# Linear attention on one core: 4 KB runs for K and V as for Q, a second matmul over 128 rows, and output one group behind

## The chip, the cores and the metric

The kernel runs on one core of one Trainium2 chip. The metric is the device time of one execution in microseconds (us), and a kernel's time is the median of several executions. The profile is one execution; its span, from the first to the last instruction, is about 1.8 us shorter than the time of the same execution. A ratio "to before" is the mean time of one kernel's runs over the mean of the other's runs of the same rounds, so it is not quite the ratio of the medians quoted beside it.

Engines: PE multiplies matrices (PEld loads its weights), DVE and ACT do elementwise work, POOL here mostly issues transfers, SP issues a few. HBM is the memory that holds the inputs and the output, SBUF the one that loads fill and stores empty, PSUM the one that PE writes its results to. A "run" of 4 KB is a contiguous stretch in HBM.

## The reference, cut to what matters

```python
# Q, K, V: 8 x 12 x 512 x 64, float32 (96 heads of 512 rows)
Q_feat = np.maximum(0, Q) + 1
K_feat = np.maximum(0, K) + 1
KV = np.einsum('bhkd,bhkv->bhdv', K_feat, V)            # first matmul
K_sum = np.sum(K_feat, axis=2)
numerator = np.einsum('bhqd,bhdv->bhqv', Q_feat, KV)    # second matmul
denominator = np.einsum('bhqd,bhd->bhq', Q_feat, K_sum)
out = numerator / (denominator[:, :, :, None] + 1e-10)
```

## The kernel before

Eight heads form a group, and there are twelve groups. Loads cast float32 to bf16 on the way. V gets a column of ones, so that the first matmul also gives the sum of K's features. Q's features are transposed on PE, and ACT copies the transposes from PSUM to SBUF (`qt`). After the second matmul DVE takes a reciprocal of the denominators and multiplies: one "pair" per PSUM tile, four pairs a group. What the argument touches (cut):

```python
def features(g):                      # DVE: K, then Q; ACT: V
    for h in range(2):
        feature(kf[:, h]..., k_raw[:, h:NP:2])
        nc.scalar.copy(out=va[:, h]..., in_=v_raw[:, h:NP:2])
    feature(qf..., q_raw)
def kv_and_transpose(g):
    # 32 matmuls over 64 rows -> kva_ps; two ACT casts to kva
    for half in range(2):
        qt_ps = psum_qt.tile([P, C, P], BF16, name="qt_ps")   # a tile for each half
        for c in range(C):
            nc.tensor.transpose(qt_ps[:, c, :], qf[:, half * C + c, :, :], identity)
        nc.scalar.copy(out=qt[:, :, :, half], in_=qt_ps)
def output(g):
    # 64 matmuls, 64 rows, 65 moving columns; four pairs of reciprocal and multiply on DVE
    ...
for it in range(NG + 2):
    if it < NG:           features(it)
    if 1 <= it < NG + 1:  kv_and_transpose(it - 1)
    if it >= 2:           output(it - 2)
    if it + IN_BUFS < NG: load(it + IN_BUFS)
    if it - LAG >= 0:     store(it - LAG)        # LAG = 3
```

Of the kernel before, what the change touches and what calls it, by code (L numbers as in the profile page):

```python
# [8 lines left out]
FP32 = mybir.dt.float32  # L9
BF16 = mybir.dt.bfloat16  # L10
ALU = mybir.AluOpType

BANK = 512
VP = 130
IN_BUFS = 4
OUT_BUFS = 6
LAG = 3


@with_exitstack  # L20
def kernel(
    ctx: ExitStack,
    tc: tile.TileContext,
    Q: bass.AP,
    K: bass.AP,
    V: bass.AP,
    out: bass.AP,
):






    nc = tc.nc

    B, H, S, D = Q.shape
    P = 128
    C = 8
    C2 = 2 * C  # L40
    NPAIR = B * H * S // (P * C)
    NP = 4
    NG = NPAIR // NP
    D1 = D + 1
    W = 2 * D + 1

    def view(t, c):
        return t.flatten_outer_dims().rearrange("(n p c) d -> p n c d", p=P, c=c)

    q_dram = view(Q, C2)  # L50
    k_dram = view(K, C)
    v_dram = view(V, C)
    o_dram = view(out, C)

    const = ctx.enter_context(tc.tile_pool(name="const", bufs=1))
    head_pool = ctx.enter_context(tc.tile_pool(name="head_pool", bufs=1))
    in_pool = ctx.enter_context(tc.tile_pool(name="in_pool", bufs=IN_BUFS))
    feat_pool = ctx.enter_context(tc.tile_pool(name="feat", bufs=2))
    mid_pool = ctx.enter_context(tc.tile_pool(name="mid", bufs=3))
    out_pool = ctx.enter_context(tc.tile_pool(name="out_pool", bufs=OUT_BUFS))  # L60
    recip_pool = ctx.enter_context(tc.tile_pool(name="recip", bufs=4))
    psum_qt = ctx.enter_context(tc.tile_pool(name="psum_qt", bufs=2, space=bass.MemoryType.PSUM))
    psum_kva = ctx.enter_context(tc.tile_pool(name="psum_kva", bufs=1, space=bass.MemoryType.PSUM))
    psum_out = ctx.enter_context(tc.tile_pool(name="psum_out", bufs=2, space=bass.MemoryType.PSUM))

    identity = const.tile([P, P], BF16, name="identity")
    NV = 2
    v_aug = [const.tile([P, 2, C, VP], BF16, name=f"v_aug{i}") for i in range(NV)]

    raw = {}  # L70
    feat = {}
    mid = {}
    outs = {}

    def load(g):
        first = g == 0
        k_raw = (head_pool if first else in_pool).tile(
            [P, NP, C, D], FP32 if first else BF16, name="k_raw"
        )
        v_raw = in_pool.tile([P, NP, C, D], BF16, name="v_raw")  # L80
        q_raw = in_pool.tile([P, 2, C2, D], BF16, name="q_raw")
        (nc.sync if first else nc.gpsimd).dma_start(  # L82
            out=k_raw, in_=k_dram[:, g * NP : g * NP + NP]
        )
        nc.gpsimd.dma_start(out=v_raw, in_=v_dram[:, g * NP : g * NP + NP])  # L85
        nc.gpsimd.dma_start(out=q_raw, in_=q_dram[:, g * 2 : g * 2 + 2])  # L86
        raw[g] = (k_raw, v_raw, q_raw)

    def store(g):
        nc.gpsimd.dma_start(out=o_dram[:, g * NP : g * NP + NP], in_=outs.pop(g))  # L90

    def feature(dst, src):
        nc.vector.tensor_scalar(  # L93
            out=dst, in0=src, scalar1=1.0, scalar2=1.0, op0=ALU.add, op1=ALU.max
        )

    def features(g):
        k_raw, v_raw, q_raw = raw.pop(g)
        kf = feat_pool.tile([P, 2, C, 2, D], BF16, name="kf")
        qf = feat_pool.tile([P, C2, 2, D], BF16, name="qf")  # L100
        va = v_aug[g % NV]
        for h in range(2):
            feature(kf[:, h].rearrange("p c n d -> p n c d"), k_raw[:, h:NP:2])
            nc.scalar.copy(  # L104
                out=va[:, h].rearrange("p c (n x) -> p n c x", n=2)[:, :, :, 0:D],
                in_=v_raw[:, h:NP:2],
            )
        feature(qf.rearrange("p c n d -> p n c d"), q_raw)
        feat[g] = (kf, qf)

    def kv_and_transpose(g):
        kf, qf = feat.pop(g)
        va = v_aug[g % NV]
        kva_ps = psum_kva.tile([P, 2, BANK], FP32, name="kva_ps")
        for h in range(2):
            for c in range(C):
                for j in range(2):
                    nc.tensor.matmul(  # L118
                        kva_ps[:, j, h * W : h * W + W],
                        lhsT=kf[64 * j : 64 * j + 64, h, c, :, :],  # L120
                        rhs=va[64 * j : 64 * j + 64, h, c, 0:W],
                        start=(c == 0),
                        stop=(c == C - 1),
                    )
        kva = mid_pool.tile([P, 2, 2, D1 + 1], BF16, name="kva")
        for n in range(2):
            nc.scalar.copy(  # L127
                out=kva[64 * n : 64 * n + 64, :, :, 0:D1],
                in_=kva_ps[64 * n : 64 * n + 64, :, 0 : 2 * W].rearrange(
                    "p j (h x) -> p j h x", h=2  # L130
                )[:, :, :, D * n : D * n + D1],
            )

        qt = mid_pool.tile([P, C, P, 2], BF16, name="qt")
        for half in range(2):
            qt_ps = psum_qt.tile([P, C, P], BF16, name="qt_ps")
            for c in range(C):
                nc.tensor.transpose(qt_ps[:, c, :], qf[:, half * C + c, :, :], identity)  # L138
            nc.scalar.copy(out=qt[:, :, :, half], in_=qt_ps)  # L139
        mid[g] = (kva, qt)  # L140

    def output(g):
        kva, qt = mid.pop(g)
        o_sb = out_pool.tile([P, NP, C, D], FP32, name="o_sb")
        for h in range(2):
            ops = [psum_out.tile([P, 2, BANK], FP32, tag="o_ps", name="o_ps") for _ in range(2)]
            for c in range(C):
                off = (c % 4) * D1
                for n in range(2):
                    for j in range(2):  # L150
                        b = 2 * h + j
                        nc.tensor.matmul(  # L152
                            ops[n][64 * j : 64 * j + 64, c // 4, off : off + D1],
                            lhsT=qt[64 * n : 64 * n + 64, c, 32 * b : 32 * b + 32, :],
                            rhs=kva[64 * n : 64 * n + 64, j, h, 0:D1],
                            start=True,
                            stop=True,
                        )
            for n in range(2):
                cells = ops[n][:, :, 0 : 4 * D1].rearrange("p b (r x) -> p b r x", x=D1)  # L160
                den = cells[:, :, :, 0:1] if n else cells[:, :, :, D:D1]
                num = cells[:, :, :, 1:D1] if n else cells[:, :, :, 0:D]
                recip = recip_pool.tile([P, 2, 4, 1], FP32, name="recip")
                nc.vector.reciprocal(out=recip, in_=den)  # L164
                nc.vector.tensor_tensor(  # L165
                    out=o_sb[:, 2 * n + h].rearrange("p (b r) d -> p b r d", b=2),
                    in0=num,
                    in1=recip.to_broadcast([P, 2, 4, D]),
                    op=ALU.mult,
                )  # L170
        outs[g] = o_sb

    with tc.manual_schedule():
        for g in range(IN_BUFS):
            load(g)
            if g == 0:
                make_identity(nc, identity)
                for t in v_aug:
                    nc.gpsimd.memset(t[:, :, :, D : D + 1], 1.0)  # L179
        for it in range(NG + 2):  # L180
            if it < NG:
                features(it)
            if 1 <= it < NG + 1:
                kv_and_transpose(it - 1)
            if it >= 2:
                output(it - 2)
            if it + IN_BUFS < NG:
                load(it + IN_BUFS)
            s = it - LAG
            if s >= 0:  # L190
                store(s)
        for s in range(NG + 2 - LAG, NG):
            store(s)


# [28 lines left out]
```

## Time and profile before

| | before |
|---|---|
| time, median of 4 | 132.04 us (130.11 to 132.31) |
| span of the profile | 129.8 us |
| busy: PE, DVE, ACT | 59.0, 57.7, 62.6 us |
| mean granted PE clock | 0.686 |

The prediction below shows the main lines. In the page's table of costliest groups the columns are line, engine, operation, output from input, count, then busy us and mean ns of one, then the idle time before them and what ended it.

```profile
L104 ACT COPY v_aug<-v_raw 128x1024 bf16<-128x1024 bf16 x24 | 24.1, 1056 | 48.6 <-DMA v_raw<-in_V_dram 48.6
...
L139 ACT COPY qt<-qt_ps 128x1024 bf16<-128x1024 bf16 x24 | 29.5, 1298 | 0.4
```

ACT stands idle 48.6 us in front of its V copies, and what ends that idle time is V's load: the engines wait for data. In front of the qt copies ACT is idle only 0.4 us in the whole kernel. The transposes that they read are nearly always there already.

### The profile page before, as it was taken

How to read it: one execution, taken by the hardware profiler on the slowest of the kernel's cores; microseconds unless marked ns; L12 is line 12 of the kernel's file. 1: busy time of each engine (PE TensorE's matmuls, PEld its weight loads, DVE VectorE, ACT ScalarE, POOL GpSimd, SP SyncE). 2: the span in 40 equal slices, each digit the busy share in tenths (PEclk: the TensorE clock that was granted, in tenths of full speed). 3: DMA queues.
4: the chain of work that ended last, by engine and by line, in shares of the span. 5: the costliest groups of instructions: out<-in, count | busy, mean ns of one | idle time of the engine just before them, and what ended most of it. 6: DMA issues, size and time to landing. Idle time of an engine off the chain costs nothing.

```text
span 129.8 us, 3048 instructions
## 1 busy us (share of the span) xinstructions
PE 59.0 (46%) x1344; PEld 50.5 (39%) x1344; DVE 57.7 (44%) x132; ACT 62.6 (48%) x73; POOL 36.1 (28%) x55
## 2 busy tenths in 40 slices
PE   0008309208758292864939119409606802933200
PEld 0007209107647191753828009308505701922100
DVE  0222212057374775727577077066227407567700
ACT  3023086590966939296690590391095096270000
POOL 6972224222332242224224222422231200202020
PEclk9999965555686959555595865875785685595555
DMA  2999999999999999999999999999999999999853
GB/s 93 321 204 195 210 194 204 210 206 211 205 209 208 209 207 206 210 207 207 277 302 207 253 331 205 231 350 191 218 347 223 212 357 418 420 417 360 341 218 121
DMA packets 19213, 32.17 MB, mean 248 GB/s; under 512 B 768, under 2 KB 12544, under 8 KB 19200
## 3 DMA queue, kind: packets, MB, share of 16 engines
q0 software_dynamic: 18672, 30.94, 106.3%
q1 hardware_dynamic: 528, 1.05, 2.1%
q8 instruction: 10, 0.16, 0.5%
q14 instruction: 3, 0.02, 0.0%
HBM read 37.75 MB, written 12.58 MB: 388 GB/s over the span
## 4 chain that ended last, share of the span: by engine, by line
DMA 72%; issue 19%; POOL 4%; POOLq 1%
DMA out_dram<-o_sb 31%; DMA k_raw<-in_K_dram 16%; DMA q_raw<-in_Q_dram 15%; DMA v_raw<-in_V_dram 9%; POOL out_dram L90 2%; POOLq L219 1%; POOL q_raw L86 1%; POOL k_raw L82 0%; POOL v_raw L85 0%; POOL identity masks.py:199 0%; POOL identity masks.py:197 0%; POOL v_aug L179 0%; POOLq L90 0%; POOLq L86 0%; POOLq L208 0%
## 5 line engine op out<-in xcount | busy, mean ns | idle before, releaser
L104 ACT COPY v_aug<-v_raw 128x1024 bf16<-128x1024 bf16 x24 | 24.1, 1056 | 48.6 <-DMA v_raw<-in_V_dram 48.6
L152 PE MATMUL o_ps<-kva,qt 64*64 64x65 bf16 x768 | 17.3, 229 | 46.9 <-DVE o_sb L165 45.8
L165 DVE TENSOR_TENSOR o_sb<-o_ps,recip 128x512 f32<-128x512 f32 x48 | 33.2, 691 | 1.6
L152 PEld LDWEIGHTS <-qt 64*64 64x64 bf16 x768 | 12.7, 137 | 52.0 <-DVE o_sb L165 48.9
L139 ACT COPY qt<-qt_ps 128x1024 bf16<-128x1024 bf16 x24 | 29.5, 1298 | 0.4
L118 PE MATMUL kva_ps<-v_aug,kf 64*128 64x129 bf16 x384 | 22.3, 302 | 15.4 <-ACT v_aug L104 10.1
L93 DVE TENSOR_SCALAR qf<-q_raw 128x2048 bf16<-128x2048 bf16 x12 | 8.3, 694 | 42.2 <-DMA q_raw<-in_Q_dram 42.2
L118 PEld LDWEIGHTS <-kf 64*128 64x128 bf16 x384 | 19.1, 137 | 16.2 <-issue 15.6
L138 PE MATMUL qt_ps<-identity,qf 128*128 128x128 bf16 x192 | 21.7, 303 | 0.1
L90 POOL DMA_DIRECT2D out_dram<-o_sb x12 | 9.3, 774 | 38.2 <-DVE o_sb L165 19.6
L138 PEld LDWEIGHTS <-qf 128*128 128x128 bf16 x192 | 18.8, 142 | 2.6 <-issue 2.2
L93 DVE TENSOR_SCALAR kf<-k_raw 128x1024 bf16<-128x1024 bf16 (+1 forms) x24 | 9.8, 450 | 11.2 <-DMA k_raw<-in_K_dram 11.1
L164 DVE RECIPROCAL recip<-o_ps 128x8 f32<-128x8 f32 x48 | 9.6, 201 | 10.5 <-PE o_ps L152 10.5
L85 POOL DMA_DIRECT2D v_raw<-in_V_dram x12 | 9.1, 759 | 17.0 <-ACT kva L127 5.4
L82 POOL DMA_DIRECT2D k_raw<-in_K_dram x11 | 8.6, 786 | 16.7 <-DVE kf L93 6.6
L86 POOL DMA_DIRECT2D q_raw<-in_Q_dram x12 | 8.4, 702 | 15.9 <-DMA k_raw<-in_K_dram 9.0
L127 ACT CAST kva<-kva_ps 64x260 bf16<-64x260 f32 x24 | 8.8, 367 | 3.5 <-PE kva_ps L118 3.4
L104 ACT ACT_TABLE_LOAD x1 | 1.3, 1283 | 0.7 <-PEq L208 0.7
masks.py:199 POOL TENSOR_SCALAR_AFFINE_SELECT identity<-identity 128x128 bf16<-128x128 bf16 x1 | 0.3, 287 | 0.1
masks.py:197 POOL MEMSET identity<- 128x128 bf16 x1 | 0.2, 244 | 0.0
L179 POOL MEMSET v_aug<- 128x16 bf16 x2 | 0.2, 175 | 0.0
L208 POOL MEMSET const-float32-0.0<- 128x1 f32 x1 | 0.1, 99 | 0.2 <-issue 0.2
(3 smaller groups left out, 0.3 us busy)
## 6 DMA issues: line engine op xcount, KB each, us to landing
out_dram<-o_sb POOLq DMA_DIRECT2D x12, 1024.0 KB, 20.0
v_raw<-in_V_dram POOLq DMA_DIRECT2D x12, 512.0 KB, 19.7
q_raw<-in_Q_dram POOLq DMA_DIRECT2D x12, 512.0 KB, 19.8
k_raw<-in_K_dram POOLq DMA_DIRECT2D x11, 512.0 KB, 19.7
k_raw<-in_K_dram SPq DMA_DIRECT2D x1, 1024.0 KB, 5.0
```

The source lines that it names most:

```text
L85: nc.gpsimd.dma_start(out=v_raw, in_=v_dram[:, g * NP : g * NP + NP])
L86: nc.gpsimd.dma_start(out=q_raw, in_=q_dram[:, g * 2 : g * 2 + 2])
L90: nc.gpsimd.dma_start(out=o_dram[:, g * NP : g * NP + NP], in_=outs.pop(g))
L93: nc.vector.tensor_scalar(out=dst, in0=src, scalar1=1.0, scalar2=1.0, op0=ALU.add, op1=ALU.max)
L104: nc.scalar.copy(out=va[:, h].rearrange("p c (n x) -> p n c x", n=2)[:, :, :, 0:D], in_=v_raw[:, h:NP:2],)
L118: nc.tensor.matmul(kva_ps[:, j, h * W : h * W + W], lhsT=kf[64 * j : 64 * j + 64, h, c, :, :], rhs=va[64 * j : 64 * j + 64, h, c, 0:W], st ...
L127: nc.scalar.copy(out=kva[64 * n : 64 * n + 64, :, :, 0:D1], in_=kva_ps[64 * n : 64 * n + 64, :, 0 : 2 * W].rearrange("p j (h x) -> p j h x ...
L138: nc.tensor.transpose(qt_ps[:, c, :], qf[:, half * C + c, :, :], identity)
L139: nc.scalar.copy(out=qt[:, :, :, half], in_=qt_ps)
L152: nc.tensor.matmul(ops[n][64 * j : 64 * j + 64, c // 4, off : off + D1], lhsT=qt[64 * n : 64 * n + 64, c, 32 * b : 32 * b + 32, :], rhs=kv ...
L164: nc.vector.reciprocal(out=recip, in_=den)
L165: nc.vector.tensor_tensor(out=o_sb[:, 2 * n + h].rearrange("p (b r) d -> p b r d", b=2), in0=num, in1=recip.to_broadcast([P, 2, 4, D]), op ...
```

## The change

Its intent: longer contiguous runs for the loads of K and V (4 KB as for Q), a second matmul that uses all 128 rows by placing two heads' weights on a block diagonal, and a shorter end, by making output one group behind instead of two and stores two behind instead of three. The core of the diff (cut and condensed; memsets and some shapes left out):

```diff
-IN_BUFS = 4
+IN_BUFS = 5
+AHEAD = 4
-LAG = 3
+LAG = 2
-    k_dram = view(K, C)
-    v_dram = view(V, C)
+    k_dram = view(K, C2)
+    v_dram = view(V, C2)
-    psum_qt, psum_kva, psum_out (2, 1 and 2 buffers)
+    psum = ctx.enter_context(tc.tile_pool(name="psum", bufs=4, space=bass.MemoryType.PSUM))
+    def keys_values(g):
+        # K features and V copies by halves, 64 matmuls over 32 rows, four casts to kva_diag
+    def queries(g):
+        qt_ps = psum.tile([P, 2, C, P], BF16, tag="ps", name="qt_ps")    # one tile for both halves
+        for half in range(2):
+            feature(qf[:, cs]..., q_raw[:, :, cs])
+            for c in range(C):
+                nc.tensor.transpose(qt_ps[:, half, c, :], qf[:, half * C + c, :, :], identity)
+            nc.scalar.copy(out=qt[:, :, :, half], in_=qt_ps[:, half])
     def output(g):
-        # lhsT=qt[64 * n : 64 * n + 64, c, ...], rhs=kva[64 * n : 64 * n + 64, j, h, 0:D1]
+        # lhsT=qt[:, c, ...], rhs=kva[:, b]  (128 rows, 130 columns, zeros off the diagonal)
-            features(it); kv_and_transpose(it - 1); output(it - 2); load(it + IN_BUFS); store(it - LAG)
+            load(g + AHEAD); store(g - LAG); keys_values(g); output(g - 1); queries(g)
```

More of the change, by code (lines that the diff above doesn't have):

```diff
@@ L13 @@
 BANK = 512
-VP = 130
-IN_BUFS = 4
+IN_BUFS = 5
 OUT_BUFS = 6
-LAG = 3
+AHEAD = 4
+LAG = 2
 @with_exitstack
@@ L44 @@
     D1 = D + 1
-    W = 2 * D + 1
+    W = 2 * D1
     def view(t, c):
@@ L61 @@
     recip_pool = ctx.enter_context(tc.tile_pool(name="recip", bufs=4))
-    psum_qt = ctx.enter_context(tc.tile_pool(name="psum_qt", bufs=2, space=bass.MemoryType.PSUM))
-    psum_kva = ctx.enter_context(tc.tile_pool(name="psum_kva", bufs=1, space=bass.MemoryType.PSUM))
-    psum_out = ctx.enter_context(tc.tile_pool(name="psum_out", bufs=2, space=bass.MemoryType.PSUM))
+    psum = ctx.enter_context(tc.tile_pool(name="psum", bufs=4, space=bass.MemoryType.PSUM))
     identity = const.tile([P, P], BF16, name="identity")
     NV = 2
-    v_aug = [const.tile([P, 2, C, VP], BF16, name=f"v_aug{i}") for i in range(NV)]
+    v_aug = [const.tile([P, C2, W], BF16, name=f"v_aug{i}") for i in range(NV)]
+    kva_diag = [const.tile([P, 4, 2, D1], BF16, name=f"kva_diag{i}") for i in range(NV)]
     raw = {}
-    feat = {}
-    mid = {}
+    qts = {}
     outs = {}
@@ L77, in load @@
         k_raw = (head_pool if first else in_pool).tile(
-            [P, NP, C, D], FP32 if first else BF16, name="k_raw"
+            [P, 2, C2, D], FP32 if first else BF16, name="k_raw"
         )
-        v_raw = in_pool.tile([P, NP, C, D], BF16, name="v_raw")
+        v_raw = in_pool.tile([P, 2, C2, D], BF16, name="v_raw")
         q_raw = in_pool.tile([P, 2, C2, D], BF16, name="q_raw")
         (nc.sync if first else nc.gpsimd).dma_start(
-            out=k_raw, in_=k_dram[:, g * NP : g * NP + NP]
+            out=k_raw, in_=k_dram[:, g * 2 : g * 2 + 2]
         )
-        nc.gpsimd.dma_start(out=v_raw, in_=v_dram[:, g * NP : g * NP + NP])
+        nc.gpsimd.dma_start(out=v_raw, in_=v_dram[:, g * 2 : g * 2 + 2])
         nc.gpsimd.dma_start(out=q_raw, in_=q_dram[:, g * 2 : g * 2 + 2])
@@ L89, in store @@
     def store(g):
-        nc.gpsimd.dma_start(out=o_dram[:, g * NP : g * NP + NP], in_=outs.pop(g))
+        o_sb = outs.pop(g)
+        o_to = o_dram[:, g * NP : g * NP + NP]
+        if g < NG - 1:
+            nc.gpsimd.dma_start(out=o_to, in_=o_sb)
+            return
+        for h in range(2):
+            nc.sync.dma_start(out=o_to[:, h:NP:2], in_=o_sb[:, h:NP:2])
     def feature(dst, src):
@@ L95, in feature @@
         )
-    def features(g):
-        k_raw, v_raw, q_raw = raw.pop(g)
-        kf = feat_pool.tile([P, 2, C, 2, D], BF16, name="kf")
-        qf = feat_pool.tile([P, C2, 2, D], BF16, name="qf")
-        va = v_aug[g % NV]
-        for h in range(2):
-            feature(kf[:, h].rearrange("p c n d -> p n c d"), k_raw[:, h:NP:2])
-            nc.scalar.copy(
-                out=va[:, h].rearrange("p c (n x) -> p n c x", n=2)[:, :, :, 0:D],
-                in_=v_raw[:, h:NP:2],
-            )
-        feature(qf.rearrange("p c n d -> p n c d"), q_raw)
-        feat[g] = (kf, qf)
@@ L111, in kv_and_transpose @@
-    def kv_and_transpose(g):
-        kf, qf = feat.pop(g)
-        va = v_aug[g % NV]
-        kva_ps = psum_kva.tile([P, 2, BANK], FP32, name="kva_ps")
-        for h in range(2):
+    def keys_values(g):
+        k_raw, v_raw, _ = raw[g]
+        kf = feat_pool.tile([P, C2, 2, D], BF16, name="kf")
+        va = v_aug[g % NV]
+        kva_ps = [psum.tile([P, 2, BANK], FP32, tag="ps", name="kva_ps") for _ in range(2)]
+        for half in range(2):
+            cs = slice(half * C, half * C + C)
+            feature(kf[:, cs].rearrange("p c n d -> p n c d"), k_raw[:, :, cs])
+            nc.scalar.copy(
+                out=va[:, cs].rearrange("p c (n x) -> p n c x", n=2)[:, :, :, 0:D],
+                in_=v_raw[:, :, cs],
+            )
+            for c in range(half * C, half * C + C):
+                for b in range(4):
+                    ps = slice(32 * b, 32 * b + 32)
+                    nc.tensor.matmul(
+                        kva_ps[b // 2][:, b % 2, 0:W],
+                        lhsT=kf[ps, c, :, :],
+                        rhs=va[ps, c, :],
+                        start=(c == 0),
+                        stop=(c == C2 - 1),
+                    )
+        kva = kva_diag[g % NV]
+        for n in range(2):
+            ps = slice(64 * n, 64 * n + 64)
+            for h in range(2):
+                nc.scalar.copy(
+                    out=kva[ps, 2 * h : 2 * h + 2, n, :],
+                    in_=kva_ps[h][ps, :, D1 * n : D1 * n + D1],
+                )
@@ new lines, in queries @@
+    def queries(g):
+        _, _, q_raw = raw.pop(g)
+        qf = feat_pool.tile([P, C2, 2, D], BF16, name="qf")
+        qt = mid_pool.tile([P, C, P, 2], BF16, name="qt")
+        qt_ps = psum.tile([P, 2, C, P], BF16, tag="ps", name="qt_ps")
+        for half in range(2):
+            cs = slice(half * C, half * C + C)
+            feature(qf[:, cs].rearrange("p c n d -> p n c d"), q_raw[:, :, cs])
+            for c in range(C):
+                nc.tensor.transpose(qt_ps[:, half, c, :], qf[:, half * C + c, :, :], identity)
+            nc.scalar.copy(out=qt[:, :, :, half], in_=qt_ps[:, half])
+        qts[g] = qt
@@ L116, in kv_and_transpose, with output @@
+    def output(g):
+        kva = kva_diag[g % NV]
+        qt = qts.pop(g)
+        o_sb = out_pool.tile([P, NP, C, D], FP32, name="o_sb")
+        for h in range(2):
+            ops = [psum.tile([P, 2, BANK], FP32, tag="ps", name="o_ps") for _ in range(2)]
             for c in range(C):
                 for j in range(2):
+                    b = 2 * h + j
                     nc.tensor.matmul(
-                        kva_ps[:, j, h * W : h * W + W],
-                        lhsT=kf[64 * j : 64 * j + 64, h, c, :, :],
@@ L121, in kv_and_transpose @@
-                        rhs=va[64 * j : 64 * j + 64, h, c, 0:W],
-                        start=(c == 0),
-                        stop=(c == C - 1),
-                    )
-        kva = mid_pool.tile([P, 2, 2, D1 + 1], BF16, name="kva")
-        for n in range(2):
-            nc.scalar.copy(
-                out=kva[64 * n : 64 * n + 64, :, :, 0:D1],
-                in_=kva_ps[64 * n : 64 * n + 64, :, 0 : 2 * W].rearrange(
-                    "p j (h x) -> p j h x", h=2
-                )[:, :, :, D * n : D * n + D1],
-            )
@@ L134, in kv_and_transpose @@
-        qt = mid_pool.tile([P, C, P, 2], BF16, name="qt")
-        for half in range(2):
-            qt_ps = psum_qt.tile([P, C, P], BF16, name="qt_ps")
-            for c in range(C):
-                nc.tensor.transpose(qt_ps[:, c, :], qf[:, half * C + c, :, :], identity)
-            nc.scalar.copy(out=qt[:, :, :, half], in_=qt_ps)
-        mid[g] = (kva, qt)
-    def output(g):
-        kva, qt = mid.pop(g)
-        o_sb = out_pool.tile([P, NP, C, D], FP32, name="o_sb")
-        for h in range(2):
-            ops = [psum_out.tile([P, 2, BANK], FP32, tag="o_ps", name="o_ps") for _ in range(2)]
-            for c in range(C):
-                off = (c % 4) * D1
-                for n in range(2):
-                    for j in range(2):
-                        b = 2 * h + j
-                        nc.tensor.matmul(
-                            ops[n][64 * j : 64 * j + 64, c // 4, off : off + D1],
-                            lhsT=qt[64 * n : 64 * n + 64, c, 32 * b : 32 * b + 32, :],
-                            rhs=kva[64 * n : 64 * n + 64, j, h, 0:D1],
-                            start=True,
-                            stop=True,
-                        )
-            for n in range(2):
-                cells = ops[n][:, :, 0 : 4 * D1].rearrange("p b (r x) -> p b r x", x=D1)
-                den = cells[:, :, :, 0:1] if n else cells[:, :, :, D:D1]
-                num = cells[:, :, :, 1:D1] if n else cells[:, :, :, 0:D]
-                recip = recip_pool.tile([P, 2, 4, 1], FP32, name="recip")
-                nc.vector.reciprocal(out=recip, in_=den)
-                nc.vector.tensor_tensor(
-                    out=o_sb[:, 2 * n + h].rearrange("p (b r) d -> p b r d", b=2),
-                    in0=num,
-                    in1=recip.to_broadcast([P, 2, 4, D]),
@@ new lines, in output @@
+                        ops[c // 4][64 * j : 64 * j + 64, c // 2 % 2, (c % 2) * W : (c % 2) * W + W],
+                        lhsT=qt[:, c, 32 * b : 32 * b + 32, :],
+                        rhs=kva[:, b],
+                        start=True,
+                        stop=True,
+                    )
+            for i in range(2):
+                cells = ops[i][:, :, 0 : 2 * W].rearrange("p b (c n x) -> p b c n x", n=2, x=D1)
+                recip = recip_pool.tile([P, 2, 2, 2, 1], FP32, name="recip")
+                nc.vector.reciprocal(out=recip, in_=cells[:, :, :, :, D:D1])
+                nc.vector.tensor_tensor(
+                    out=o_sb[:, h:NP:2, 4 * i : 4 * i + 4].rearrange(
+                        "p n (b c) d -> p b c n d", b=2
+                    ),
+                    in0=cells[:, :, :, :, 0:D],
+                    in1=recip.to_broadcast([P, 2, 2, 2, D]),
@@ L173 @@
     with tc.manual_schedule():
-        for g in range(IN_BUFS):
+        for g in range(AHEAD):
             load(g)
@@ L177 @@
                 make_identity(nc, identity)
+                for t in kva_diag:
+                    nc.gpsimd.memset(t, 0.0)
                 for t in v_aug:
-                    nc.gpsimd.memset(t[:, :, :, D : D + 1], 1.0)
-        for it in range(NG + 2):
-            if it < NG:
-                features(it)
-            if 1 <= it < NG + 1:
-                kv_and_transpose(it - 1)
-            if it >= 2:
-                output(it - 2)
-            if it + IN_BUFS < NG:
-                load(it + IN_BUFS)
-            s = it - LAG
-            if s >= 0:
-                store(s)
-        for s in range(NG + 2 - LAG, NG):
-            store(s)
+                    nc.gpsimd.memset(t[:, :, D::D1], 1.0)
+        for g in range(NG):
+            if g + AHEAD < NG:
+                load(g + AHEAD)
+            if g >= LAG:
+                store(g - LAG)
+            keys_values(g)
+            if g:
+                output(g - 1)
+            queries(g)
+        output(NG - 1)
+        for g in range(NG - LAG, NG):
+            store(g)
 _INS = ['Q', 'K', 'V']
```

## The prediction

> **What bounds the kernel now.** I read the page first: busy shares, the forty slices, the chain; then the DMA queue's timeline, the timeline of one group, the waits.
>
> ```profile
> PE 59.0 (46%) x1344; PEld 50.5 (39%) x1344; DVE 57.7 (44%) x132; ACT 62.6 (48%) x73; POOL 36.1 (28%) x55
> ...
> DMA  2999999999999999999999999999999999999853
> GB/s 93 321 204 195 210 194 204 210 206 211 205 209 208 209 207 206 210 207 207 277 302 207 253 331 205 231 350 191 218 347 223 212 357 418 420 417 360 341 218 121
> ...
> DMA 72%; issue 19%; POOL 4%; POOLq 1%
> ```
>
> No engine is busy half the span, while the DMA row is full from the second slice to the thirty-seventh. GB/s counts the bf16 side of a load, so 205 to 210 is 410 to 420 GB/s read from HBM, what the pure stores at the end show (417 to 420). The chain is DMA for 72%. The kernel runs at the transfer rate.
>
> Next, whether long runs are faster. K and V (L82, L85) have 2 KB runs in HBM, Q (L86) already has the 4 KB runs that the change gives K and V:
>
> ```profile
> 30.38 0.70 POOL L86 DMA_DIRECT2D q_raw<-in_Q_dram  x1 [1.78 <-DMA k_raw<-in_K_dram]
> 33.00 0.77 POOL L82 DMA_DIRECT2D k_raw<-in_K_dram  x1 [1.93 <-DVE kf L93]
> 35.46 0.74 POOL L85 DMA_DIRECT2D v_raw<-in_V_dram  x1 [1.69 <-ACT kva L127]
> 37.96 0.70 POOL L86 DMA_DIRECT2D q_raw<-in_Q_dram  x1 [1.76 <-DMA k_raw<-in_K_dram]
> 40.50 0.77 POOL L82 DMA_DIRECT2D k_raw<-in_K_dram  x1 [1.84 <-DVE kf L93]
> ```
>
> Issues go out about 2.5 us apart, each when the transfer eight before it lands. In the trace's landings a K or V load advances the queue by 2.55 us on its first engine, a Q load by 2.48, a store by 2.51. Per group that is 7.6 us with loads alone and 10.1 us with a store.
>
> Last, what one group costs the engines:
>
> ```profile
> 8.92 2.01 ACT L104 COPY v_aug<-v_raw 128x1024 bf16<-128x1024 bf16 x2 [6.90 <-DMA v_raw<-in_V_dram]
> ...
> 10.12 1.92 PE L118 MATMUL kva_ps<-v_aug,kf 64*128 64x129 bf16 x32 [10.12 <-ACT v_aug L104]
> ...
> 26.86 2.45 ACT L139 COPY qt<-qt_ps 128x1024 bf16<-128x1024 bf16 x2
> ...
> 28.05 0.20 DVE L164 RECIPROCAL recip<-o_ps 128x8 f32<-128x8 f32 x1
> 28.28 0.69 DVE L165 TENSOR_TENSOR o_sb<-o_ps,recip 128x512 f32<-128x512 f32 x1
> 28.89 0.20 DVE L164 RECIPROCAL recip<-o_ps 128x8 f32<-128x8 f32 x1
> ...
> 32.30 1.89 PE L138 MATMUL qt_ps<-identity,qf 128*128 128x128 bf16 x16
> ```
>
> and from the list of waits (us in total, times, longest):
>
> ```profile
> ACT v_aug L104 <- DMA v_raw<-in_V_dram: 48.6, 12, 6.9
> ...
> DVE qf L93 <- DMA q_raw<-in_Q_dram: 42.2, 12, 5.4
> ```
>
> The columns are start, us, engine, line, operation, count. A reciprocal and its multiply repeat every 0.84 us. ACT has 5.2 us of work a group and DVE 4.8, below the transfers' 7.6, and both wait on loads in every group. They can, because before works on three groups at once: features of one, first matmul and transposes of the previous, output of the one before that. So no chain runs through all engines within one iteration.
>
> **What the Trainium skill says.** "DMA: Bandwidth & Descriptors", "Where 436 GB/s comes from", gives a fabric ceiling of 435 GB/s and says that for HBM transfers the HBM side binds at about 358. The trace agrees with the first (a 1 MB store in 2.51 us is 418), not the second. "PSUM — Partial Sum Buffer", "Engine vs sequencer instructions": ScalarE and VectorE queues are strict FIFO and matmuls complete in program order. The trace agrees: each engine's order is the program's. "TensorEngine Tiling (Array Packing)", "Key Properties": tiles can load weights and multiply in parallel. Two 64-row matmuls of 129 columns start every 108 ns here, and four 64x64 ones of 65 columns in 55, so a set costs its columns once; four 32-row tiles no run has shown yet. "TensorE: Matmul & The Clock Gate", "What's actually happening": the clock is halved by default and a window of about 3.4 us of activity releases it. Here the clock records step in 3.41 us between 0.5 and 1.0, mean 0.69.
>
> **The change part by part.** (a) 4 KB runs: at best 23 loads x (2.55 - 2.48) = 1.6 us, and only while the transfers bound. (b) First matmul: 64 instead of 32 a group, over 32 rows and 130 columns. If four share the array, 16 sets x 0.108 = 1.7 us, as now. (c) Second matmul: 32 instead of 64 a group, but two share the array over 130 columns rather than four over 65: 16 x 0.108 = 1.7 us instead of 0.9. (d) ACT: four casts of 130 elements instead of two of 260, some 0.3 us more; DVE: Q's features in two halves, 0.1 us more. (e) The last store leaves in two halves from SP, and seven stores instead of eight follow the last load. At most the tail's gain is 0.7 us: the next-to-last store lands at 125.0 and 2.5 more would be 127.5, against 128.2 now.
>
> None of this is large. What matters is (f), the order. In the changed program each iteration runs features and first matmul of g, output of g-1, then features, transposes and copies of Q of g; the order of instructions confirms it on all three engines. Follow it round. ACT's V copies of g+1 stand behind its qt copies of g; those need the transposes; those need Q's features, which on DVE stand behind all four reciprocal-multiply pairs of output g-1; those need the second matmul, which on PE stands behind the first matmul of g; and that needs ACT's V copies of g. The loop closes once per group, and everything on it is serial. At half clock:
>
> - V copies 2.01, and 0.13 to PE (first copy done near 9.97, matmul at 10.12);
> - second half of the first matmul, 8 sets x 0.108 = 0.87 (the first half hides behind the second copy), a PE drain 0.20 (the idle time before the transposes in the PE rows);
> - second matmul up to the first PSUM tile, 4 pairs x 0.108 + 0.13 to come out = 0.56;
> - four pairs on DVE 4 x 0.84 = 3.36, the first half of Q's features 0.42;
> - 0.06 to PE, 8 transposes x 0.107 + 0.10 = 0.95, 0.09 to ACT (hops as in before: DVE end 109.84 to PE 109.90, PE end 112.40 to ACT 112.49);
> - two qt copies 2.45.
>
> Sum 11.1 us, and 10.0 if PE had full clock all the time (0.43 + 0.22 + 0.43 off). PE's bursts become 3.7 and 1.8 us with 2.5 to 3 us idle between, so a 3.4 us window is seldom full, and I expect more half clock than now: 10.9. That is above the 10.1 of the transfers, so the loop takes over as the bound.
>
> The total: group 1 starts when V of 1 lands, 16.5 as now. Eleven turns x 10.9 = 119.9, to 136.4. Last output 0.2 + 0.56 + 3.36 + 0.1 = 4.2, to 140.6. Half a store: 1.25 of data plus about 2.4 fixed (K's first load took 5.0 for 2.5 of data), to 144.3. End of program 1.5 (128.2 to 129.8), so 145.8; plus the 1.7 between the profiled run's time (131.5) and its span: 147.
>
> **Rivals.** One, the transfers stay the bound: then (a) and (e) give 1.6 + 0.7 and the time is about 129 to 130. For it: loads may run four groups ahead, and no engine's busy time exceeds 6 us a group. Against: busy time is not the question in a loop; pure ACT and DVE work on it is already 8.2 us, and with PE at full clock and the hops 10.0. Two, the loop at full clock: 10.0 a turn gives 137 to 138. For it: PE stays active with shorter gaps than now. Three, worse: four row tiles do not share the array, or weight loads limit (64 a group). Each half of the first matmul then takes up to 1.7 instead of 0.87, both halves show beyond the first copy, a turn costs about 1.5 more, and the time is about 164. Against: 64x64 weights issue 14 ns apart in the trace.
>
> **Range and chances.** The start and the tail are known within 2 us; the turn is multiplied by eleven, so 10.0 to 11.4 spans 138 to 153, my range. To be within 2% of 132 the turn would have to be below 9.7, under the full-clock sum. Slower 0.87, same 0.06, faster 0.07; the last is for an overlap that I have overlooked.
>
> **What would show it.** The DMA row should fall below nine after the first third, and the chain should change from DMA to DVE, ACT and PE. ACT's V copies should no longer wait on the V load but come straight after the qt copies, about 11 us apart; DVE should wait on PE and PE on DVE and ACT each group; mean clock nearer 0.5 to 0.6. If the DMA row stays full and the V copies still wait on loads, the loop argument is wrong. If the turn is right and the time is not, the start or the tail is.

## The result

| | before | after |
|---|---|---|
| time, median of 4 | 132.04 us | 157.65 us (157.47 to 157.74) |
| ratio to before | | 1.203 (1.188 to 1.218) |
| span of the profile | 129.8 us | 155.8 us |
| busy: PE, DVE, ACT | 59.0, 57.7, 62.6 us | 68.6, 58.3, 65.3 us |
| mean granted PE clock | 0.686 | 0.618 |

The changed kernel is 20% slower. The prediction had said slower, at 147, and the time lies above its range (138 to 153).

The page of the changed kernel, same rows as before: busy times, forty slices of PE, DMA and GB/s, and the chain of what ended last.

```profile
PE 68.6 (44%) x1344; PEld 58.7 (38%) x1344; DVE 58.3 (37%) x144; ACT 65.3 (42%) x97; POOL 35.5 (23%) x56
...
DMA  4999999999999999999999999999910600700715
GB/s 149 270 212 210 211 211 211 211 211 212 210 212 210 210 343 195 260 295 200 328 220 223 330 211 296 261 217 381 399 61 38 231 4 0 269 4 0 269 56 213
...
PE 32%; DVE 28%; ACT 18%; issue 10%; DMA 7%; POOL 2%; POOLq 0%
```

The DMA row is full only until slice 29. After that come single stores with nothing between them (269, 4, 0), because the loads are done, and each store has to wait for its output. The loads run up to four groups ahead and kept the row full until then: POOL issued the last of them at 88.26 us, and with the median of 19.4 us from issue to landing it landed near 107.7. The chain has turned from 72% DMA to PE, DVE and ACT in turn, with DMA at 7%. Busy time has hardly grown: ACT by 2.7 us, DVE by 0.6, PE by 9.6, against a span that grew by 26. The kernel is not busier; it waits more.

One turn of the loop, in order of time (start, us, engine, line, operation, count, and in brackets idle time before it and what ended it). The PE clock was at half for all of this turn:

```profile
87.63 2.00 ACT L109 COPY v_aug<-v_raw 128x1024 bf16<-128x1024 bf16 x2
...
88.74 2.00 PE L116 MATMUL kva_ps<-v_aug,kf 32*128 32x130 bf16 x64 [2.30 <-ACT v_aug L109]
...
90.67 2.00 PE L154 MATMUL o_ps<-kva_diag,qt 128*64 128x130 bf16 x32
...
91.36 0.21 DVE L164 RECIPROCAL recip<-o_ps 128x8 f32<-128x8 f32 x1 [6.98 <-PE o_ps L154]
...
94.73 0.75 DVE L97 TENSOR_SCALAR qf<-q_raw 128x1024 bf16<-128x1024 bf16 x2
...
95.20 1.03 PE L141 MATMUL qt_ps<-identity,qf 128*128 128x128 bf16 x8 [2.53 <-DVE qf L97]
...
96.27 1.29 ACT L142 COPY qt<-qt_ps 128x1024 bf16<-128x1024 bf16 x1 [4.57 <-PE qt_ps L141]
97.62 1.01 PE L141 MATMUL qt_ps<-identity,qf 128*128 128x128 bf16 x8 [1.38 <-ACT qt L142]
...
98.67 1.29 ACT L142 COPY qt<-qt_ps 128x1024 bf16<-128x1024 bf16 x1 [1.10 <-PE qt_ps L141]
99.82 2.00 ACT L109 COPY v_aug<-v_raw 128x1024 bf16<-128x1024 bf16 x2
```

Read the brackets as links. V copies release the first matmul, which is followed by the second, which releases DVE after 6.98 us idle; DVE's four pairs end in Q's features, which release PE; PE releases ACT after 4.57 us idle; and after its two copies ACT starts the next V copies, 12.19 us after the last ones. The prediction had drawn this ring. It had not drawn the link in the last four lines: the second eight transposes start only when the first copy has ended (1.38 <-ACT qt), and the second copy then waits 1.10 us for them. In the kernel before, all idle time in front of these copies was 0.4 us.

The list of waits says the same in total (us, times, longest). Before, the first of these three was 10.5 us and the other two were not in the list; DVE's and ACT's longest waits were for loads:

```profile
DVE recip L164 <- PE o_ps L154: 81.3, 12, 7.4
ACT qt L142 <- PE qt_ps L141: 61.1, 23, 4.6
...
PE qt_ps L141 <- ACT qt L142: 15.2, 11, 1.4
```

The V copies of group 1 start at 15.57 and those of group 11 at 135.56: ten turns of 12.00 us.

### The profile page after: what moved, and what is told of

Its sections match the earlier page's. It is cut to its first block, busy times and chain, and to the rows that moved or that the text cites. A ratio compares the mean times of both kernels' runs of the same rounds, so it can differ in the third digit from the quotient of the medians. Undisturbed runs are those within 1.5% of the kernel's fastest.

```text
span 155.8 us, 3110 instructions
## 1 busy us (share of the span) xinstructions
PE 68.6 (44%) x1344; PEld 58.7 (38%) x1344; DVE 58.3 (37%) x144; ACT 65.3 (42%) x97; POOL 35.5 (23%) x56
## 3 DMA queue, kind: packets, MB, share of 16 engines
HBM read 37.75 MB, written 12.58 MB: 323 GB/s over the span
## 4 chain that ended last, share of the span: by engine, by line
PE 32%; DVE 28%; ACT 18%; issue 10%; DMA 7%; POOL 2%; POOLq 0%
DVE o_sb L165 21%; PE kva_ps L116 14%; PE qt_ps L141 13%; ACT qt L142 10%; ACT v_aug L109 8%; DMA v_raw<-in_V_dram 7%; PE o_ps L154 5%; DVE recip L164 5%; DVE qf L97 3%; POOL kva_diag L181 1%; POOL q_raw L84 0%; POOL v_raw L83 0%; POOL k_raw L80 0%; POOL v_aug L183 0%; POOL identity masks.py:199 0%
## 5 line engine op out<-in xcount | busy, mean ns | idle before, releaser
L142 ACT COPY qt<-qt_ps 128x1024 bf16<-128x1024 bf16 x24 | 31.0, 1292 | 61.1 <-PE qt_ps L141 61.1
L164 DVE RECIPROCAL recip<-o_ps 128x8 f32<-128x8 f32 x48 | 9.6, 200 | 81.3 <-PE o_ps L154 81.3
L116 PE MATMUL kva_ps<-v_aug,kf 32*128 32x130 bf16 x768 | 23.9, 306 | 34.9 <-ACT v_aug L109 34.9
L141 PEld LDWEIGHTS <-qf 128*128 128x128 bf16 x192 | 17.2, 130 | 49.5 <-DVE qf L97 31.2
L116 PEld LDWEIGHTS <-kf 32*128 32x128 bf16 x768 | 20.7, 136 | 37.6 <-issue 36.7
L154 PE MATMUL o_ps<-kva_diag,qt 128*64 128x130 bf16 x384 | 23.5, 310 | 1.4 <-ACT qt L142 1.4
L154 PEld LDWEIGHTS <-qt 128*64 128x64 bf16 x384 | 20.7, 166 | 3.8 <-issue 2.2
L127 ACT CAST kva_diag<-kva_ps 64x130 bf16<-64x130 f32 x48 | 10.3, 264 | 14.6 <-PE kva_ps L116 14.3
L97 DVE TENSOR_SCALAR kf<-k_raw 128x1024 bf16<-128x1024 bf16 (+1 forms) x24 | 11.0, 500 | 7.4 <-DMA k_raw<-in_K_dram 7.4
L97 DVE TENSOR_SCALAR qf<-q_raw 128x1024 bf16<-128x1024 bf16 x24 | 9.2, 425 | 3.5 <-DMA q_raw<-in_Q_dram 3.5
L181 POOL MEMSET kva_diag<- 128x520 bf16 x2 | 1.0, 527 | 0.0
## 6 DMA issues: line engine op xcount, KB each, us to landing
v_raw<-in_V_dram POOLq DMA_DIRECT2D x12, 512.0 KB, 19.4
q_raw<-in_Q_dram POOLq DMA_DIRECT2D x12, 512.0 KB, 19.4
```

What stands on the lines that cost most here:

```text
L97: nc.vector.tensor_scalar(out=dst, in0=src, scalar1=1.0, scalar2=1.0, op0=ALU.add, op1=ALU.max)
L116: nc.tensor.matmul(kva_ps[b // 2][:, b % 2, 0:W], lhsT=kf[ps, c, :, :], rhs=va[ps, c, :], start=(c == 0), stop=(c == C2 - 1),)
L127: nc.scalar.copy(out=kva[ps, 2 * h : 2 * h + 2, n, :], in_=kva_ps[h][ps, :, D1 * n : D1 * n + D1],)
L141: nc.tensor.transpose(qt_ps[:, half, c, :], qf[:, half * C + c, :, :], identity)
L142: nc.scalar.copy(out=qt[:, :, :, half], in_=qt_ps[:, half])
L154: nc.tensor.matmul(ops[c // 4][64 * j : 64 * j + 64, c // 2 % 2, (c % 2) * W : (c % 2) * W + W], lhsT=qt[:, c, 32 * b : 32 * b + 32, :], r ...
```

## The experiments

Theory: the order within an iteration closes a ring through ACT, PE and DVE, which sets the time; the shared PSUM tile `qt_ps` is the term of about 1.1 us a turn that the prediction left out. Rivals: the work itself (the larger second matmul, 32-row tiles, four casts) is too slow; DVE's place in the queue is not what closes the ring; the longer runs hurt the transfers.

### Two PSUM tiles for the two halves

```diff
-        qt_ps = psum.tile([P, 2, C, P], BF16, tag="ps", name="qt_ps")
         for half in range(2):
+            qt_ps = psum.tile([P, 2, C, P], BF16, tag="ps", name="qt_ps")
...
-                nc.tensor.transpose(qt_ps[:, half, c, :], qf[:, half * C + c, :, :], identity)
-            nc.scalar.copy(out=qt[:, :, :, half], in_=qt_ps[:, half])
+                nc.tensor.transpose(qt_ps[:, 0, c, :], qf[:, half * C + c, :, :], identity)
+            nc.scalar.copy(out=qt[:, :, :, half], in_=qt_ps[:, 0])
```

> The changed kernel, but each half of the transposes writes a PSUM tile of its own, so that the second eight transposes need not wait for the copy of the first eight. Theory (a serial loop through all engines, and the shared tile is the term the prediction left out): each turn loses the idle time of 1.1 us between the two copies on ACT, 12.0 to about 10.9 us; 157.6 - 11 x 1.1 = about 145 us. Rival 1 (the doubled second matmul or the slower clock is what was left out): no change, 156 to 158. Rival 2 (transfers): no change.

Measured: 143.37 us (4 runs), 1.092 of before. ACT's timeline:

```profile
58.03 2.01 ACT L109 COPY v_aug<-v_raw 128x1024 bf16<-128x1024 bf16 x2
...
66.75 2.45 ACT L142 COPY qt<-qt_ps 128x1024 bf16<-128x1024 bf16 x2 [4.64 <-PE qt_ps L141]
69.05 2.02 ACT L109 COPY v_aug<-v_raw 128x1024 bf16<-128x1024 bf16 x2
```

The two qt copies now run back to back in 2.45 us, with no idle time between them. The turn here is 11.02 us and 10.70 in the mean of ten, against the 10.9 predicted for the changed kernel. Taking the shared tile away brought 14.3 us, more than the 12 or so expected, and a kernel without it comes out 3.6 us under the prediction's 147, inside its range. Not all of the 14.3 us is the wait itself: at half clock a turn lost 1.17 us (12.19 to 11.02), 12.9 in eleven turns. In the mean it lost 1.30 (12.00 to 10.70); the granted clock was also higher (mean 0.670 against 0.618), which may be the rest.

### Queries before output

```diff
             keys_values(g)
+            queries(g)
             if g:
                 output(g - 1)
-            queries(g)
```

> The changed kernel with one line moved: the work on Q of group g comes before the output of group g-1. Everything else of the change stays. Theory (the order closes the loop): DVE's four pairs (3.4 us) and the second matmul leave the loop, a turn would be about 8.0 us, less than the 10 us that the transfers of a group take, so the transfers bind again: 128 to 131 us, the row of DMA full, V copies waiting on loads. Rival (the work itself is too slow: 32-row tiles, doubled matmul, four casts, a PSUM pool of four shared tiles): stays above 145.

Measured: 130.41 us (129.36 to 131.19), 0.993 of before. With everything else of the change in place, the order alone takes back 27 us. The row of DMA:

```profile
DMA  3999999999999999999999999999999999999395
```

It is full but for one slice near the end, where the store of group 10 waits for its output. With this order, both of the last outputs come after the last queries. Part of the expectation failed: the V copies wait on V's load only twice, and the turn was 9.2 us, not 8.0. The first matmul waits for K's features instead (23.4 us in ten waits), which stand behind the pairs on DVE. That is a shorter ring, but still one.

### Second matmul over 64 rows

```diff
-                        ops[c // 4][64 * j : 64 * j + 64, c // 2 % 2, (c % 2) * W : (c % 2) * W + W],
-                        lhsT=qt[:, c, 32 * b : 32 * b + 32, :],
-                        rhs=kva[:, b],
+                        ops[n][64 * j : 64 * j + 64, c // 4, (c % 4) * D1 : (c % 4) * D1 + D1],
+                        lhsT=qt[64 * n : 64 * n + 64, c, 32 * b : 32 * b + 32, :],
+                        rhs=kva[64 * n : 64 * n + 64, b, n, :],
```

(and the pairs' views of PSUM to match)

> The changed kernel with the second matmul as before, 64 over 64 rows and 64 columns of weights with 65 moving columns in place of 32 over 128 rows with 130. Theory (DVE's pairs follow the first PSUM tile, and what PE does after it is hidden behind them): the first tile is ready at about the same time (0.65 against 0.6 us), 156 to 159 us. Rival (the doubled second matmul is what costs): PE's time for it falls from 2.0 to about 1.1 us a turn, 0.9 x 12 = 11 us less, about 147.

Measured: 159.36 us, 1.213 of before. PE's timeline in one turn:

```profile
79.84 0.66 PE L154 MATMUL o_ps<-kva_diag,qt 64*64 64x65 bf16 x32
...
80.76 0.83 PE L154 MATMUL o_ps<-kva_diag,qt 64*64 64x65 bf16 x32 [0.26 <-ACT kva_diag L127]
```

The second matmul went from 2.00 us a turn to 1.5 (0.66 + 0.83; I had expected 1.1), and the kernel did not get faster. Its turn was 12.23 us in the mean, like the 12.19 of the changed kernel at half clock; in the profiled run its clock was released even less (mean 0.549). What PE does after the first PSUM tile is hidden behind DVE's pairs. The larger matmul is ruled out as the cause.

### Q's features early on DVE

```diff
     def queries(g):
         ...
         for half in range(2):
-            cs = slice(half * C, half * C + C)
-            feature(qf[:, cs].rearrange("p c n d -> p n c d"), q_raw[:, :, cs])
             for c in range(C):
                 nc.tensor.transpose(qt_ps[:, half, c, :], qf[:, half * C + c, :, :], identity)
...
             keys_values(g)
+            query_features(g)        # the two feature instructions taken out of queries(g)
             if g:
                 output(g - 1)
             queries(g)
```

> The changed kernel with the features of Q of group g made on DVE before DVE's part of output g-1; transposes and copies stay where they are, behind the second matmul on PE. Theory: only DVE's 3.4 us of pairs and 0.4 of features leave the loop, PE's whole second matmul (2.0 instead of 0.6) enters it: 2.0 + 0.1 + 0.9 + 0.2 + 1.75 + 0.2 + 0.95 + 0.1 + 1.3 + 1.1 + 1.3 = 9.9 us a turn, about the transfers' 10: 134 to 140 us. If DVE's place in its queue is not what closes the loop: no change, 157.

Measured: 127.60 us (127.53 to 127.67), 0.972 of before (0.968 to 0.977). Two instructions moved in DVE's queue made the slow kernel faster than the one before. The page:

```profile
DMA  3999999999999999999999999999999999999992
GB/s 85 335 212 209 212 211 212 210 212 212 212 210 211 212 212 212 210 318 272 204 275 316 203 241 352 209 217 358 223 207 343 244 213 313 417 419 413 417 391 79
```

The row of DMA is full to the thirty-ninth slice. The time was below what I expected (134 to 140). I had added the last output and store to a ring of 9.9 us; the turn was 9.06 in the mean (9.59 in the turn from 60.89, whose transposes all ran at half clock, and 8.56 in the next, where they ran faster), so DVE was done at 119.8 us, while the transfers still in the queue ran to 124.9 and hid the rest. DVE's place in its queue does close the ring.

### Early features and two tiles

The same two edits as above in one kernel.

> The kernel with Q's features made early, and the two halves of the transposes in PSUM tiles of their own as well. Theory: with Q's features early the transfers already bind (row of DMA full to the last slice), so the 1.1 us a turn that brought some 14 us in the serial loop brings nothing here: 127 to 128.5 us. Rival (the loop, about 9 us a turn, still sets the end there): 1.1 us x 11 off, or at least 3 us less than 127.6.

Measured: 128.52 us (6 runs), 0.9717 of before, in another set of rounds in which before took 132.46; the kernel without the second tile had 0.9721. The edit that was worth 14 us in the ring is worth nothing once the transfers bind.

### The transfers alone, with 2 KB and with 4 KB runs

Both take the kernel before, drop all computation and store one constant tile (a wrong result). The second has this edit as well:

```diff
-    k_dram = view(K, C)
-    v_dram = view(V, C)
+    k_dram = view(K, C2)
+    v_dram = view(V, C2)
```

> Wrong result on purpose: only the loads and stores of the kernel before, in its order and with its 2 KB runs for K and V; every store sends one constant tile and nothing is computed. This is the floor of the transfers: 47 transfers of about 2.52 us after the first load, 126 to 128 us. If the kernel before loses time other than by transfers, it is that much above this.

> Wrong result on purpose: the same with 4 KB runs for K and V, the part (a) of the change by itself. Theory from the landings (2.55 against 2.48 us per load): 23 x 0.05 to 0.07 = 1.2 to 1.6 us less than with 2 KB runs. Rival (runs of 2 KB are already as fast, the difference came from engine skew): the same within 0.3 us.

Measured: 130.01 us (129.29 to 130.60, 6 runs) with 2 KB runs and 128.78 (128.70 to 129.04) with 4 KB, in the same rounds. The 2 KB floor was 2 us above what I expected, since 126 to 128 had left out the 1.8 us between span and time. The difference, 1.23 us, is within what part (a) was estimated at (at best 1.6). The kernel before, at 132.46 us in these rounds, stood about 2.4 us above its own transfers: a ratio of 0.982 (0.977 to 0.987), which the 2% rule leaves unclear. So it ran near the transfer rate, not quite at it. The kernel with early features stands at 0.972 of before, and the transfers alone with 4 KB runs at 0.974. These are the transfers in the order of the kernel before, with its longer end, and in other rounds; still, no time above its transfers can be seen in that kernel.

### The changed order alone, in the kernel before

```diff
             if it < NG:
                 features(it)
+                kv(it)                # features of K and V, first matmul, casts
             if 1 <= it < NG + 1:
-                kv_and_transpose(it - 1)
-            if it >= 2:
-                output(it - 2)
+                output(it - 1)
+            if it < NG:
+                queries(it)           # features, transposes and copies of Q
```

> The kernel before with the changed order alone: features and first matmul of K and V of g, output of g-1, then features, transposes and copies of Q of g. Its 2 KB runs, 64-row matmuls, separate PSUM pools and separate tiles for the two halves of the transposes stay. Theory (the order is the cause): a turn is 2.0 + 0.1 + 0.9 + 0.2 + 0.8 + 4.2 (its pairs with two waits for PSUM) + 0.4 + 0.1 + 0.95 + 0.1 + 2.45 = about 12.2 us, so 152 to 160 us. Rival (the larger matmuls and the shared pool slow the changed kernel): 130 to 134 us.

Measured: 161.93 us, 1.225 of before, a little above the range of 152 to 160. Before's own matmuls, runs, pools and separate tiles are all there; the order alone makes it slower than the changed kernel. A turn is 12.02 us, and from its timeline:

```profile
85.02 1.89 PE L141 MATMUL qt_ps<-identity,qf 128*128 128x128 bf16 x16 [2.44 <-DVE qf L93]
86.09 2.45 ACT L142 COPY qt<-qt_ps 128x1024 bf16<-128x1024 bf16 x2 [5.81 <-PE qt_ps L141]
...
88.39 2.02 ACT L103 COPY v_aug<-v_raw 128x1024 bf16<-128x1024 bf16 x2
```

The copies run in one go, since this kernel has two tiles for the two halves. Its turn is as long for two other reasons. DVE's four pairs took 4.2 us (80.11 to 84.28 in that turn, from the first reciprocal to Q's features) instead of 3.37, and Q's features are one instruction here, so that the transposes start 0.74 us after its start instead of 0.47. Together that is 1.07 us, about the 1.10 of the shared tile. As to the pairs, its pool for output holds two tiles where a group needs four, so PE waits for DVE and then DVE for PE, as the expectation had it.

## Why the prediction was wrong

The direction, the mechanism and the evidence named for it held. The chain went from DMA to DVE, ACT and PE; the DMA row emptied, though from slice 30 on and not after the first third; the V copies followed the qt copies without waiting on their load. The ring is shown as cause by three runs: queries first (27 us back), DVE's two instructions early (30 us back), and the order alone in the kernel before (29.5 us lost).

The step that failed is a term of the sum for one turn: "two qt copies 2.45". Terms as predicted at half clock, and the turn shown above that ran wholly at half clock:

| from | to | predicted | measured |
|---|---|---|---|
| V copies start | second matmul starts | 2.01 + 0.13 + 0.87 + 0.20 = 3.21 | 90.67 - 87.63 = 3.04 |
| second matmul | first reciprocal | 0.56 | 91.36 - 90.67 = 0.69 |
| four pairs | Q's features start | 3.36 | 94.73 - 91.36 = 3.37 |
| Q's features | transposes start | 0.42 + 0.06 = 0.48 | 95.20 - 94.73 = 0.47 |
| transposes | first qt copy | 0.95 + 0.09 = 1.04 | 96.27 - 95.20 = 1.07 |
| first qt copy | next V copies | 2.45 | 99.82 - 96.27 = 3.55 |
| sum | | 11.10 | 12.19 |

All terms but the last agree, within 0.2 us singly and 0.01 in their sum. The last is 1.10 too small, 12.1 us in eleven turns: I took the second eight transposes to hide behind the first copy, as they do in the kernel before. There each half has a PSUM tile of its own; in the changed kernel both halves share one, and the program makes PE wait until ACT has read the first half before it writes the second. The halves are at different bytes, so no data requires this. Two tiles took it away, and the result was correct. The wait stood in the changed program's instruction order, at the first transpose of the second half, before any run. I used that order to draw the ring and did not check each wait on it.

In the total, with the prediction's parts: the start came 0.9 earlier (15.57 against 16.5), eleven turns took 132.3 instead of 119.9 (15.57 to 147.9, where the last copy ends), the last output took the 4.2 predicted, the last half store 2.8 instead of 3.7 (152.1 to 154.9), the end 0.9 instead of 1.5. That is 12.4 - 0.9 - 0.9 - 0.6 = 10.0 more than the parts' sum of 147.5 (145.8 + 1.7), and the time of the profiled run is 157.6. The smaller errors at the start and the end, 2.4 us together, happened to make the miss smaller; that was luck.

The other points. (a) The 4 KB runs brought 1.2 us to the transfers alone, inside the 1.6 estimated; that they bring nothing to the changed kernel, where the transfers no longer bind, is argued and not tested. (b) Four 32-row tiles share the array as assumed: 64 matmuls of 130 columns took 2.00 us. (c) The second matmul grew to 2.00 us a turn and cost nothing, as the sum implied. (d) ACT's casts grew by 0.12 us a group instead of the 0.3 allowed (10.3 us in all against 8.8), Q's features by 0.08 (9.2 against 8.3). (e) The end is not tested by a run of its own. The clock was expected near 0.5 to 0.6 and was 0.618. It mattered little: the turn that began at 75.86, in which the first eight transposes ran faster (0.62 instead of 1.03), took 11.77 us. Of the rivals, the first (transfers stay the bound) and the second (full clock) fell; the third (four row tiles do not share the array) would have given about 164, near the time but for a wrong reason, and the first matmul's 2.00 us rules it out.

One thing stays open: how the gain of 4.0 us of the best kernel (131.60 to 127.60) splits. By the transfer kernels, 1.2 us is the 4 KB runs, and about 2.4 us is what the kernel before lost above its own transfers. What the new order and the shorter end each took of these 2.4 us is not known, since no run undid the end alone.

## What to carry to other kernels

Busy shares below 50% on every engine don't say that an engine order is safe: before changing the order of stages, follow each engine's queue round from one iteration to the same point of the next, and compare the length of that ring with what bounds the kernel now. When you lengthen a ring, go through every wait on it, including those for PSUM tiles that two halves of a stage share. To break a ring it can be enough to move a cheap instruction or two ahead in its engine's queue: two features of 0.4 us each, moved ahead of four pairs, took 30 us off.

## What the Trainium skill lacked or had wrong

- "DMA: Bandwidth & Descriptors", "Where 436 GB/s comes from": its sentence that the HBM side binds HBM transfers at about 358 GB/s does not name its condition, and the prediction found the trace at odds with it. With one core running, the stores of the best kernel moved at 413 to 419 GB/s (its slices 35 to 38), and the reads and writes of its whole span come to 400 GB/s (37.75 + 12.58 MB in 125.8 us). The skill does not lack the answer: a note under the table just above, in "Measured (HBM→SBUF, 128 partitions, SWDGE, issued from GpSimd)", gives about 358 as each core's part when both cores of an HBM domain stream, which no run here did.
- "Perfetto Trace Analysis", "Optimization Strategy": it says that consistent bubbles can mean too little SBUF or PSUM for the next tile. Here DVE stood idle about 7 us in each of eleven turns. With two instructions moved in its queue and the same pools, its idle time before the reciprocals fell from 81.3 to 38.8 us, and the kernel was 30 us faster. The page, which goes on to the semaphores that an instruction waits on, could name the order of an engine's queue as a second cause.
- No page that I read says that two halves of one tile can be serialized by the program though they share no byte. The wait here was 1.1 us a turn, and taking the shared tile away brought 14.3 us in all.
- "TensorE: Matmul & The Clock Gate", "What's actually happening": its halved default agrees: the page of the kernel with the second matmul over 64 rows shows half clock in every slice from the fifth on. "Seeing it yourself" there warns that clock events in a trace can be unreliable. What it lacks is that the mean granted clock can mislead too. The kernel before in the changed order showed a mean of 1.00 in its profile, while its 16 transposes took 1.89 us, as long as at half clock elsewhere; the trace held no clock record at all, and the mean seems to count a time without records as full clock.
